# A joint gate/up block's products in a fixed order, a longer trail for the second token half, and a new buffer layout in both feed-forward phases

## The chip, the cores and the metric

The kernel runs on one core of one Trainium2 chip, as a single launch. The metric is the device time of the launch in microseconds (us). The engines named below are TensorE (PE: the matmuls; PEld: its weight loads), VectorE (DVE), ScalarE (ACT), GpSimd (POOL) and SyncE (SP, which here issues the loads of weights). Each engine runs its own instructions in a fixed order; an instruction that has to wait holds up those behind it on the same engine. DMA transfers run beside them.

## The reference

One decoder layer on 256 tokens of width 2048, in float32:

```
x <- LN1(alpha*x + 0.5*SwiGLU_1(x))                  # FFN 1, inner width 5632
x <- LN2(alpha*x + W_out [DiffAttn(x) || RWKV7(x)])  # the mixers
x <- LN3(alpha*x + 0.5*SwiGLU_2(x))                  # FFN 2, inner width 5632
swiglu(x) = (silu(x @ w_gate) * (x @ w_up)) @ w_down
```

`alpha` is 2 to the power 1/4, and each LN is a layer norm with gain and bias over the 2048 columns. The change does not touch the inside of the mixers.

## The kernel before

**Split numbers.** Each float32 factor is split into a high part in the matmul's format (fp32r) and the rest, the low part. A product of one 128-row piece of weights with one token half (128 tokens, 512 output columns) is three matmuls that add into the same bank: high x high, high x low, low x high (L130, L131, L132). The halves of the tokens are transposed and kept as `xh`, `xl`; those of the inner activations as `hh`.

**A tile of weights.** SP loads up to three 128-row pieces as `raw` (L114; 8 buffers in an FFN). ACT casts them to the high part `wh` (L122), and DVE subtracts to get the low part `wl` (L123). There are NW pairs of `wh`/`wl` buffers, 4 in an FFN, used in turn. A cast into a buffer waits until PE has finished the last product that reads it.

**Plain blocks.** `Stream.block` streams the tiles of 512 output columns. The first token half's product runs as a tile arrives; the second half's product trails by LAG tiles (`pend`), one tile in an FFN. The first block of gate and of up, and all of the down projection, run so. Each FFN is worked off in two parts over the inner width: six and five column blocks of gate and up, then four column blocks of down over them.

**Joint blocks.** The other ten column blocks of gate and up in each FFN run in `two_blocks`, which computes gate and up for both token halves together and saves products over the first six pieces by a scheme of sums and differences (Winograd's). The sums of activations for it (`comb`, tiles `xs`, `xsh`, `xsl`) are made once per FFN by `combinations`, L284 to L292. A joint block opens with six products of nine matmuls each. They are called P1 to P6 below, in the order of the code:

- P1 (L170): bank a, from tile r11 of the gate weights.
- P2 (L173): bank z, from the difference r12 - r11 that DVE makes in place (L172).
- P3 (L178): bank u, which ACT has filled with a copy of a (L174), from r22 less that difference (DVE, L177).
- P4 (L183): bank a again, from r21.
- P5 (L185): bank w, which ACT has filled with a copy of u after P3 (L181), from r22 - r12 (DVE, L176).
- P6 (L187): bank u again, after DVE has added s5, a copy of z, to it (L184).

After them come the other ten pieces in plain form, each tile for both token halves. There are 20 joint blocks. Four of them open a stretch: the first of each half of each FFN. The other 16 follow another joint block and are called ordinary.

**Norms.** When a down block of the second half ends, DVE adds it to `y` (L351) and takes statistics (L352). After the fourth, `ln_tail` aggregates them (L240), applies the norm in two passes of four pieces (L248, L249), and PE transposes each piece through a bank `tr` (L76), or DMA stores it (L251 at the end; L254 for the residual).

**Order.** The code is recorded and then put in order by a list scheduler that simulates the engines. It may move an instruction ahead of others on its engine as far as data and buffers allow; what it decides is fixed in the program.

Of the kernel before, what the change touches and what calls it, by code (L numbers as in the profile page):

```python
# [10 lines left out]
F32 = mybir.dt.float32  # L11
# [5 lines left out]
P = 128  # L17
# [12 lines left out]
SCALE = 64 ** -0.5  # L30
LAG = {"ffn": 1, "mix": 2}
NW = {"ffn": 4, "mix": 5}
# [8 lines left out]
def build(tc, A, out):  # L41
# [31 lines left out]
    def transpose_split(src, tt, q, store, on_dve=False):  # L73
        tr = tr_bank[-1]()
# [15 lines left out]
    class Stream:  # L90
# [9 lines left out]
        def phase(self, name, pool, banks=None):  # L100
            assert not self.pend
            self.name, self.pool, self.banks, self.slot, self.rot = name, pool, banks, 0, 0
            self.wide = WIDE[name]

# [12 lines left out]
        def halves(self, raw, n, w=NB, g=None):  # L117
            wh, wl = (self.pool.tile([P, self.wide, NB], F32R, tag=f"{t}{self.slot}", name=nm(t)) for t in ("wh", "wl"))
            self.slot = (self.slot + 1) % NW[self.name]
            for k in range(0, n, g or n):  # L120
                c = slice(k, k + (g or n))
                SC.copy(out=wh[:, c, :w], in_=raw[:, c, :w])  # L122
                V.tensor_tensor(out=wl[:, c, :w], in0=raw[:, c, :w], in1=wh[:, c, :w].bitcast(F32), op=ALU.subtract)  # L123
            return wh, wl

        def product(self, acc, lhs, n, wh, wl, first, last, w=NB):
            a = acc[:, :w]
            for j in range(n):
                hi, lo = lhs(j)
                T.matmul(a, hi, wh[:, j, :w], start=first and j == 0, stop=False, skip_group_check=True)  # L130
                T.matmul(a, hi, wl[:, j, :w], start=False, stop=False, skip_group_check=True)  # L131
                T.matmul(a, lo, wh[:, j, :w], start=False, stop=last and j == n - 1, skip_group_check=True)  # L132

# [10 lines left out]
        def block(self, src, c0, w, ks, lhs, done, wide=None):  # L144
            blk = dict(ks=ks, w=w, lhs=lhs, done=done)
            wide = wide or self.wide
            ki = 0
            while ki < len(ks):
                left = len(ks) - ki
                n = wide if left % wide == 0 or left > 2 * wide else min(2, left)  # L150
                for f in self.hooks.get(self.step, ()):
                    f()
                self.step += 1
                g = 1 if self.step == 1 else None
                raw = self.load(src, ks[ki][0], n, c0, w, g)
                st = (blk, ki, n) + self.halves(raw, n, w, g)
                self.mm(st, 0)
                self.pend.append(st)
                if len(self.pend) > max(0, min(LAG[self.name], self.step // 4 - 1)):
                    self.mm(self.pend.pop(0), 1)  # L160
                self.run_bg()
                ki += n

        def two_blocks(self, srcs, c0, x, comb, done):
# [12 lines left out]
            V.tensor_tensor(out=r11, in0=r22, in1=r11, op=ALU.subtract)  # L177
            self.product(u, comb(1), 3, *self.halves(r11, 3), False, False)  # L178
            s5 = self.pool.tile([P, NB], F32, tag="s5", name=nm("s5"))
            SC.copy(out=s5, in_=z)  # L180
            SC.copy(out=w, in_=u)  # L181
            r21 = self.load(s0, 3, 3, c0)
            self.product(a, A12, 3, *self.halves(r21, 3), False, False)  # L183
            V.tensor_tensor(out=u, in0=u, in1=s5, op=ALU.add)  # L184
# [87 lines left out]
    def ffn(fp, wg, wu, wd, lg, lb, res, last, extra=None):  # L272
# [5 lines left out]
        def combinations():  # L278
# [10 lines left out]
            V.tensor_tensor(out=sr[:, 3], in0=x12, in1=sr[:, 1], op=ALU.subtract)  # L289
            sh, sl = (fp.tile([P, 4, 3, P], F32R, tag=t, name=nm(t)) for t in ("xsh", "xsl"))  # L290
            SC.copy(out=sh, in_=sr)
            V.tensor_tensor(out=sl, in0=sr, in1=sh.bitcast(F32), op=ALU.subtract)  # L292
            return lambda i: lambda j: (sh[:, i, j, :], sl[:, i, j, :])
        for half, nj in enumerate((6, 5)):
# [118 lines left out]
    def mix(mp, pq, C):  # L413
# [567 lines left out]
    def ffn_bank(pool):  # L981
        return lambda: pool.tile([P, 4, P], F32, tag="tr", name=nm("tr"), bufs=2)

    with tc.tile_pool(name="fp1", bufs=1, reuse_waits="tile") as fp, tc.tile_pool(name="pt1", bufs=1, space=bass.MemoryType.PSUM, reuse_waits="tile") as pt:
        tr_bank.append(ffn_bank(pt))
        stream.phase("ffn", fp, pt)
        xc = [fp.tile([P, D], F32, tag=f"y{tt}", name=nm("xc")) for tt in range(2)]

# [59 lines left out]
```

## Time and profile before

| | |
|---|---|
| three runs | 2017.73 us median, 2016.71 to 2018.85 |
| the profiled execution | 2017.31 us, of which the span from first to last instruction is 2015.2 |
| mean granted TensorE clock | 0.983 of full |
| PE, PEld, DVE, ACT, POOL busy | 96%, 79%, 68%, 48%, 2% of the span |
| matmuls, weight loads | 9491 each |
| read from memory | 364 MB, at 184 GB/s over the span |

A row of the timeline gives the start in us from the span's start, the time it took, the engine, the line of the program, the operation with its output and inputs, the size, the number of instructions taken together, and in brackets how long the engine had been idle before it and what released it. A row of the waits gives the total, the number of times and the longest, in us. A row of the windows gives the stretch, its length, the busy time of PE, PEld, DVE, ACT and POOL with their instruction counts, the granted TensorE clock, the share of the DMA engines' time, and GB/s. A matmul's time in a row is from start to end, while the next begins earlier; the distance of starts is what a stream of them takes.

### The profile page before, as it was taken

What the parts mean: (1) busy time and instruction counts of PE and PEld (TensorE: products, weight loads), DVE (VectorE), ACT (ScalarE), POOL (GpSimd) and SP (SyncE); (2) the same over time, 40 slices, a digit from 0 to 9 for tenths busy, and PEclk for the clock granted to TensorE, in tenths of its full rate; (3) what the DMA queues carried; (4) which work ended last, traced back from release to release, by engine and by line L of the source; (5) the groups of instructions that cost most, each with busy time, mean ns of one, the idle gap of its engine ahead of it and who ended that gap; (6) DMA issues with size and microseconds to landing.
All of it is one profiled execution on the core that took longest, in us unless ns stands there. A gap on an engine that the chain in (4) does not pass through costs nothing. (4 is left out here: it accounts for less than half of the span.)

```text
span 2015.2 us, 24059 instructions
## 1 busy us (share of the span) xinstructions
PE 1944.6 (96%) x9491; PEld 1585.4 (79%) x9491; DVE 1377.2 (68%) x1477; ACT 971.0 (48%) x1078; POOL 43.5 (2%) x76
## 2 busy tenths in 40 slices
PE   9999999999999989999999988899999999999997
PEld 7787888887888868877778766778878888878885
DVE  6888744578775565776777768667885447888455
ACT  5565543355554325645574543445554334555431
POOL 0200000000000000000000000000000000000000
PEclk9999999999999979999999999889999999999998
DMA  9546566545667426555445634855457565456851
GB/s 323 180 168 208 198 246 218 174 167 199 203 201 264 147 91 193 166 152 164 130 133 161 185 131 127 277 165 172 167 191 258 206 212 177 167 180 206 268 193 42
DMA packets 200465, 373.27 MB, mean 185 GB/s; under 512 B 20778, under 2 KB 22896, under 8 KB 200096
## 3 DMA queue, kind: packets, MB, share of 16 engines
q1 hardware_dynamic: 180688, 350.52, 52.0%
q10 hardware_dynamic: 17440, 14.29, 2.5%
q0 software_dynamic: 2224, 6.93, 1.3%
q8 instruction: 74, 1.21, 0.2%
q14 instruction: 39, 0.32, 0.0%
HBM read 364.10 MB, written 7.60 MB: 184 GB/s over the span
## 5 line engine op out<-in xcount | busy, mean ns | idle before, releaser
L123 DVE TENSOR_TENSOR wl<-raw,wh 128x1536 fp32r<-128x1536 f32 (+3 forms) x585 | 881.8, 1522 | 511.9 <-ACT wh L122 510.0
L122 ACT CAST wh<-raw 128x1536 fp32r<-128x1536 f32 (+3 forms) x585 | 750.7, 1294 | 802.4 <-PE acc L132 638.0
L131 PE MATMUL acc<-wl,xh 128*128 128x512 f32 (+1 forms) x1652 | 644.2, 392 | 6.4 <-DVE wl L123 6.4
L132 PE MATMUL acc<-wh,xl 128*128 128x512 f32 (+1 forms) x1652 | 641.4, 390 | 0.0
L130 PE MATMUL acc<-wh,xh 128*128 128x512 f32 (+1 forms) x1652 | 636.0, 393 | 3.1 <-ACT wh L122 3.1
L131 PEld LDWEIGHTS acc<-wl,xh 128*128 128x128 f32 x1652 | 312.0, 189 | 72.6 <-DVE wl L123 8.3
L130 PEld LDWEIGHTS acc<-wh,xh 128*128 128x128 f32 x1652 | 312.4, 189 | 69.9 <-ACT wh L122 4.9
L132 PEld LDWEIGHTS acc<-wh,xl 128*128 128x128 f32 x1652 | 312.1, 189 | 64.6 <-issue 1.7
L131 PE MATMUL acc<-wl,hh 128*128 128x512 f32 x704 | 274.4, 390 | 0.0
L132 PE MATMUL acc<-wh,hh 128*128 128x512 f32 x704 | 274.2, 390 | 0.0
L130 PE MATMUL acc<-wh,hh 128*128 128x512 f32 x704 | 270.1, 389 | 0.0
L131 PEld LDWEIGHTS acc<-wl,hh 128*128 128x128 f32 x704 | 132.1, 188 | 27.5
L132 PEld LDWEIGHTS acc<-wh,hh 128*128 128x128 f32 x704 | 132.2, 188 | 27.3
L130 PEld LDWEIGHTS acc<-wh,hh 128*128 128x128 f32 x704 | 132.1, 188 | 27.2
L130 PE MATMUL acc<-wh,xsh 128*128 128x512 f32 x240 | 100.6, 419 | 14.6 <-ACT acc L181 13.2
L131 PE MATMUL acc<-wl,xsh 128*128 128x512 f32 x240 | 95.4, 398 | 3.6 <-DVE wl L123 3.6
L132 PE MATMUL acc<-wh,xsl 128*128 128x512 f32 x240 | 95.2, 397 | 0.0
L130 PEld LDWEIGHTS acc<-wh,xsh 128*128 128x128 f32 x240 | 45.8, 191 | 35.7 <-ACT acc L181 21.9
L131 PEld LDWEIGHTS acc<-wl,xsh 128*128 128x128 f32 x240 | 46.1, 192 | 12.8 <-DVE wl L123 4.4
L132 PEld LDWEIGHTS acc<-wh,xsl 128*128 128x128 f32 x240 | 46.0, 192 | 10.3
L300 ACT ACTIVATE sg<-acc 128x512 f32<-128x512 f32 x44 | 26.2, 599 | 20.3 <-PE acc L132 20.2
L172 DVE TENSOR_TENSOR raw<-raw,raw 128x1536 f32<-128x1536 f32 x20 | 35.2, 1758 | 0.7
(263 smaller groups left out, 1104.1 us busy)
## 6 DMA issues: line engine op xcount, KB each, us to landing
raw<-in_ffn_w_down_dram SPq DMA_DIRECT2D x112, 768.0 KB, 4.3
raw<-in_ffn_w_up_dram SPq DMA_DIRECT2D x88, 768.0 KB, 6.2
raw<-in_ffn_w_gate_dram SPq DMA_DIRECT2D x80, 768.0 KB, 6.4
raw<-in_w_in_dram SPq DMA_DIRECT2D x96, 512.0 KB, 3.6
raw<-in_ffn_w_gate_dram SPq DMA_DIRECT2D x55, 512.0 KB, 4.7
raw<-in_ffn_w_up_dram SPq DMA_DIRECT2D x44, 512.0 KB, 5.2
raw<-in_w_out_dram SPq DMA_DIRECT2D x32, 512.0 KB, 3.8
raw<-in_ffn_w_down_dram SPq DMA_DIRECT2D x8, 512.0 KB, 3.6
```

The source lines that it names most:

```text
L122: SC.copy(out=wh[:, c, :w], in_=raw[:, c, :w])
L123: V.tensor_tensor(out=wl[:, c, :w], in0=raw[:, c, :w], in1=wh[:, c, :w].bitcast(F32), op=ALU.subtract)
L130: T.matmul(a, hi, wh[:, j, :w], start=first and j == 0, stop=False, skip_group_check=True)
L131: T.matmul(a, hi, wl[:, j, :w], start=False, stop=False, skip_group_check=True)
L132: T.matmul(a, lo, wh[:, j, :w], start=False, stop=last and j == n - 1, skip_group_check=True)
L172: V.tensor_tensor(out=r11, in0=r12, in1=r11, op=ALU.subtract)
L300: SC.activation(out=s, in_=acc, func=AF.Silu)
```

## The change

- `two_blocks`: the order edge `tc.issue_after(i)` puts P4's matmuls behind the last matmul of P3. The casts and differences are recorded as before.
- `LAG` in an FFN is 2 instead of 1. In the first gate and up block's gate part, and in the down projection of the second half, it is 3, with 5 pairs of `wh`/`wl` buffers instead of 4. The trail builds up by one tile for every two steps at the start.
- FFN 2's first gate block uses tiles three pieces wide, not two.
- `ffn_layout` claims the FFN's buffers in one given order (raw, combination halves, s5, sg, h, y) before any is used, which moves them; the split combinations get tags of their own.
- Two of three transposes of a norm use a spare accumulator bank in place of the two `tr` banks.

```
-LAG = {"ffn": 1, "mix": 2}
+LAG = {"ffn": 2, "mix": 2}
...
-                if len(self.pend) > max(0, min(LAG[self.name], self.step // 4 - 1)):
+                while len(self.pend) > max(0, min(self.lag, (self.step - 1) // 2)):
                     self.mm(self.pend.pop(0), 1)
...
-            self.product(u, comb(1), 3, *self.halves(r11, 3), False, False)
+            i = self.product(u, comb(1), 3, *self.halves(r11, 3), False, False)
...
             r21 = self.load(s0, 3, 3, c0)
-            self.product(a, A12, 3, *self.halves(r21, 3), False, False)
+            h = self.halves(r21, 3)
+            with tc.issue_after(i):
+                self.product(a, A12, 3, *h, False, False)
...
-                    stream.block(wg, c0, NB, KX, x_lhs, gate_done, 2)
+                    stream.buffers(5, 3)
+                    stream.block(wg, c0, NB, KX, x_lhs, gate_done, 3 if last else 2)
+                    stream.buffers(4, 2)
...
             if half == 1:
                 gb = load_gb_over_x(lg, lb)
+                stream.buffers(5, 3)
...
+        def bank(spare=False):
+            n[0] += 1
+            if spare and n[0] % 3:
+                i = (stream.rot + n[0] % 3) % NACC["ffn"]
+                return (pa if i < 3 else pool).tile([P, 4, P], F32, tag=f"acc{i}", name=nm("tr"))
+            return pool.tile([P, 4, P], F32, tag="tr", name=nm("tr"), bufs=2)
...
+    def ffn_layout(fp):
+        for tag, n in (("raw", NRAW["ffn"]), ("wh4", 1), ("wl4", 1)):
+            fp.tile([P, 3, NB], F32, tag=tag, name=nm(tag), bufs=n)
+        for tag, n in (("s5", 1), ("sg", 2), ("h", 2)):
+            fp.tile([P, NB], F32, tag=tag, name=nm(tag), bufs=n)
+        for t in range(2):
+            fp.tile([P, D], F32, tag=f"y{t}", name=nm("y"))
```

The lines that the prediction names move by a few: L122 and L123 become L125 and L126, L130 to L132 become L133 to L135, L172, L177, L181, L184 and L188 become L176, L181, L185, L190 and L194, L351 becomes L360, L284 becomes L290.

PE in an ordinary joint block (the second of FFN 1), from the transposes that stand between P2 and P3. Before; `wh_153` is P3's tile and `wh_157` P4's:

```order
L308 MATMUL tr_137_774<-ident_73,h_136_772 128x128 x4
L308 MATMUL tr_140_790<-ident_73,h_139_788 128x128 x4
L130 MATMUL acc_143_799<-wh_153_838,xsh_58_327 128x512
L130 MATMUL acc_141_797<-wh_157_856,xh_6_98 128x512
L131 MATMUL acc_141_797<-wl_158_857,xh_6_98 128x512
L132 MATMUL acc_141_797<-wh_157_856,xl_7_99 128x512
```

The changed program at the same place; `wh_161` is P3's tile:

```order
L314 MATMUL tr_145_782<-ident_73,h_144_780 128x128 x4
L314 MATMUL tr_148_798<-ident_73,h_147_796 128x128 x4
L133 MATMUL acc_151_807<-wh_161_846,wh4_66_323 128x512
L134 MATMUL acc_151_807<-wl_162_847,wh4_66_323 128x512
L135 MATMUL acc_151_807<-wh_161_846,wl4_67_324 128x512
L133 MATMUL acc_151_807<-wh_161_846,wh4_66_323 128x512
```

Before, P4 starts after one matmul of P3, and the other eight follow it; now all nine of P3 stand before P4. DVE's and ACT's rows of this block, from the cast of its first tile to the addition to u, are in the same order in both programs.

DVE in FFN 1's first joint block, from L177 on. Before; `wl_103` belongs to P4, `wl_105` to P5, `wl_99` to P3, `wl_107` to P6:

```order
L177 TENSOR_TENSOR raw_91_497<-raw_97_529,raw_91_497 128x1536
L123 TENSOR_TENSOR wl_103_552<-raw_101_549,wh_102_551 128x1536
L123 TENSOR_TENSOR wl_105_566<-raw_94_512,wh_104_565 128x1536
L319 TENSOR_TENSOR hh_83_468<-tr_82_463,hh_83_468 128x512
L123 TENSOR_TENSOR wl_99_534<-raw_91_497,wh_98_533 128x1536
L123 TENSOR_TENSOR wl_107_580<-raw_97_529,wh_106_579 128x1536
```

The change; `wl_111` belongs to P4, `wl_113` to P5, `wl_115` to P6 and `wl_107` to P3:

```order
L126 TENSOR_TENSOR wl_111_560<-raw_109_557,wh_110_559 128x1536
L325 TENSOR_TENSOR hh_91_467<-tr_90_462,hh_91_467 128x512
L181 TENSOR_TENSOR raw_99_505<-raw_105_537,raw_99_505 128x1536
L126 TENSOR_TENSOR wl_113_574<-raw_102_520,wh_112_573 128x1536
L325 TENSOR_TENSOR hh_91_467<-tr_93_493,hh_91_467 128x512
L126 TENSOR_TENSOR wl_115_588<-raw_105_537,wh_114_587 128x1536
L126 TENSOR_TENSOR wl_107_542<-raw_99_505,wh_106_541 128x1536
```

P3's low half moved from before P6's to behind it, while on PE P3 moved ahead of P4 as above.

DVE in the first joint block of FFN 1's second half, from L177 on. Before; `wl_496`, `wl_492`, `wl_498` belong to P4, P3, P5:

```order
L177 TENSOR_TENSOR raw_484_2877<-raw_490_2909,raw_484_2877 128x1536
L349 SCALAR_TENSOR_TENSOR y_365_2021<-rc_478_2868,acc_458_2701 128x512
L123 TENSOR_TENSOR wl_496_2932<-raw_494_2929,wh_495_2931 128x1536
L123 TENSOR_TENSOR wl_492_2914<-raw_484_2877,wh_491_2913 128x1536
L123 TENSOR_TENSOR wl_498_2946<-raw_487_2892,wh_497_2945 128x1536
```

The change; `wl_504`, `wl_506`, `wl_500` belong to P4, P5, P3:

```order
L358 SCALAR_TENSOR_TENSOR y_373_2029<-rc_486_2876,acc_469_2724 128x512
L181 TENSOR_TENSOR raw_492_2885<-raw_498_2917,raw_492_2885 128x1536
L126 TENSOR_TENSOR wl_504_2940<-raw_502_2937,wh_503_2939 128x1536
L126 TENSOR_TENSOR wl_506_2954<-raw_495_2900,wh_505_2953 128x1536
L126 TENSOR_TENSOR wl_500_2922<-raw_492_2885,wh_499_2921 128x1536
```

P3's low half now stands behind P5's. FFN 2's second half has the same rows in the same order, and FFN 2's first joint block has P3's low half behind P6's in both programs. On PE, the matmuls between the last use of the buffer that a block's first tile goes into and that block's P1 are 41 before and 27 now in FFN 1's first joint block, 45 and 36 in the first of each second half, 33 and 32 in FFN 2's first, and 42 and 42 in an ordinary one. After the last product of the first token half, 14 matmuls of the second follow before a norm, and now 22.

More of the change, by code (lines that the diff above doesn't have):

```diff
@@ L73, in transpose_split @@
     def transpose_split(src, tt, q, store, on_dve=False):
-        tr = tr_bank[-1]()
+        tr = tr_bank[-1](True)
         for j in range(4):
@@ L102, in phase, with buffers @@
             self.name, self.pool, self.banks, self.slot, self.rot = name, pool, banks, 0, 0
-            self.wide = WIDE[name]
+            self.wide, self.lag, self.nw = WIDE[name], LAG[name], NW[name]
+        def buffers(self, nw, lag):
+            self.nw, self.lag, self.slot = nw, lag, self.slot % nw
         def bank(self):
@@ L118, in halves @@
             wh, wl = (self.pool.tile([P, self.wide, NB], F32R, tag=f"{t}{self.slot}", name=nm(t)) for t in ("wh", "wl"))
-            self.slot = (self.slot + 1) % NW[self.name]
+            self.slot = (self.slot + 1) % self.nw
             for k in range(0, n, g or n):
@@ L131, in product @@
                 T.matmul(a, hi, wl[:, j, :w], start=False, stop=False, skip_group_check=True)
-                T.matmul(a, lo, wh[:, j, :w], start=False, stop=last and j == n - 1, skip_group_check=True)
+                i = T.matmul(a, lo, wh[:, j, :w], start=False, stop=last and j == n - 1, skip_group_check=True)
+            return i.ins
         def mm(self, st, tt):
@@ L289, in combinations @@
             V.tensor_tensor(out=sr[:, 3], in0=x12, in1=sr[:, 1], op=ALU.subtract)
-            sh, sl = (fp.tile([P, 4, 3, P], F32R, tag=t, name=nm(t)) for t in ("xsh", "xsl"))
+            sh, sl = (fp.tile([P, 4, 3, P], F32R, tag=t, name=nm(t)) for t in ("wh4", "wl4"))
             SC.copy(out=sh, in_=sr)
@@ L947, in mix, with mix_bank @@
         rot = [0]
-        def mix_bank():
+        def mix_bank(spare=False):
             rot[0] += 1
@@ L981, in ffn_bank @@
     def ffn_bank(pool):
-        return lambda: pool.tile([P, 4, P], F32, tag="tr", name=nm("tr"), bufs=2)
+        n = [0]
+        def bank(spare=False):
[4 more added lines that the diff above has]
+            return pool.tile([P, 4, P], F32, tag="tr", name=nm("tr"), bufs=2)
+        return bank
+    def ffn_layout(fp):
[5 more added lines that the diff above has]
+            fp.tile([P, D], F32, tag=f"y{t}", name=nm("y"))
     with tc.tile_pool(name="fp1", bufs=1, reuse_waits="tile") as fp, tc.tile_pool(name="pt1", bufs=1, space=bass.MemoryType.PSUM, reuse_waits="tile") as pt:
@@ L986, in build @@
         stream.phase("ffn", fp, pt)
+        ffn_layout(fp)
         xc = [fp.tile([P, D], F32, tag=f"y{tt}", name=nm("xc")) for tt in range(2)]
@@ L1007, in build @@
         stream.phase("ffn", fp, pt)
+        ffn_layout(fp)
         ffn(fp, A["ffn2_w_gate"][0], A["ffn2_w_up"][0], A["ffn2_w_down"][0], A["ln3_g"], A["ln3_b"], xs, True)
```

## The prediction, made before the changed kernel was run

> **What bounds the kernel now.** I read the page's busy shares first, then the waits, then the timeline of one joint block.
>
> ```profile
> PE 1944.6 (96%) x9491; PEld 1585.4 (79%) x9491; DVE 1377.2 (68%) x1477; ACT 971.0 (48%) x1078; POOL 43.5 (2%) x76
> ...
> PE acc L130 <- ACT acc L181: 13.2, 20, 0.7
> ...
> 1985.02 0.39 PE L132 MATMUL acc<-wh,hh 128*128 128x512 f32 x1
> ...
> 1994.54 0.39 PE L132 MATMUL acc<-wh,hh 128*128 128x512 f32 x1
> ```
>
> TensorE (PE) is busy 96% of the span, so whatever moves the time must move PE's idle time or its clock. The third line says that in each of the 20 joint blocks PE stands 0.66 us (13.2 over 20) for the copy of u into w. The last two rows are 42 matmuls apart: 9.52 / 42 = 0.227 us a matmul, so a nine-matmul product takes 2.04 us. The share does not say what ends second there. In the joint block at 90 to 112 us:
>
> ```profile
> 89.88 1.48 ACT L122 CAST wh<-raw 128x1536 fp32r<-128x1536 f32 x1 [1.03 <-PE acc L132]
> 91.39 1.76 DVE L123 TENSOR_TENSOR wl<-raw,wh 128x1536 fp32r<-128x1536 f32 x1 [2.17 <-ACT wh L122]
> 93.18 1.76 DVE L172 TENSOR_TENSOR raw<-raw,raw 128x1536 f32<-128x1536 f32 x1
> 94.97 1.76 DVE L176 TENSOR_TENSOR raw<-raw,raw 128x1536 f32<-128x1536 f32 x1
> ...
> 98.32 0.68 DVE L305 SCALAR_TENSOR_TENSOR h<-sg,acc 128x512 f32<-128x512 f32 x1
> 98.92 1.75 DVE L177 TENSOR_TENSOR raw<-raw,raw 128x1536 f32<-128x1536 f32 x1
> 101.18 5.09 DVE L123 TENSOR_TENSOR wl<-raw,wh 128x1536 fp32r<-128x1536 f32 x3
> 106.19 1.75 DVE L188 TENSOR_TENSOR raw<-raw,raw 128x1536 f32<-128x1536 f32 x1
> 110.73 0.68 DVE L184 TENSOR_TENSOR acc<-acc,s 128x512 f32<-128x512 f32 x1
> 109.10 0.50 PE L130 MATMUL acc<-wh,xsh 128*128 128x512 f32 x1 [0.66 <-ACT acc L181]
> 111.47 0.19 PEld L130 LDWEIGHTS acc<-wh,xsh 128*128 128x128 f32 x1 [0.22 <-DVE acc L184]
> ```
>
> The cast of the block's first tile starts when PE frees its buffer. From then VectorE (DVE) runs without a stop until the addition u += s5 at L184 ends at 111.41, and P6, which needs it, loads its weights at 111.47 after waiting 0.22 us. So PE waits twice, and the second wait is the end of a full DVE queue. From the rows: 1.51 us from the cast to the first difference, 1.79 for each of the next two steps, then 1.67 for a wide operation (101.18 to 106.19 is three) and 0.60 for a narrow one (98.32 to 98.92).
>
> **The edge in the 16 ordinary joint blocks.** The copy now runs under P4, and PE is spared that stop: 0.66 us idle and the slower restart (0.50 for the first matmul, not 0.39 as at 1985.02), an estimate of 0.8 in all. But DVE's and ScalarE's (ACT's) orders between cast and L184 are as before, and 42 matmuls stand between the freed buffer and P1 both times. P6 can start no earlier than 111.5, so PE waits there for what it no longer waits before P5. Gain: nothing I can price; bounds -0.2 us a block (the 0.22 above) and +0.3 (a second restart, since the one stop becomes two, before P3's low half and before P6). I take 0, and -3 to +5 for all 16.
>
> **The edge in the four opening blocks.** There DVE has the low half of P3 after P4's and P5's (in the first block of each FFN after P6's too). Before, P4 could fill PE meanwhile; now P3 has to come first, and P4, P5 and P6 stand in PE's queue behind it. The second FFN's first block has this DVE order already before the change:
>
> ```profile
> 1309.16 1.48 ACT L122 CAST wh<-raw 128x1536 fp32r<-128x1536 f32 x1 [3.02 <-PE acc L132]
> ...
> 1326.55 1.75 DVE L123 TENSOR_TENSOR wl<-raw,wh 128x1536 fp32r<-128x1536 f32 x1
> ...
> 1328.35 0.80 PE L131 MATMUL acc<-wl,xsh 128*128 128x512 f32 x1 [2.77 <-DVE wl L123]
> ...
> 1337.22 0.61 PE L130 MATMUL acc<-wh,xsh 128*128 128x512 f32 x1
> ```
>
> P3's low half was ready 19.14 us after the cast (1328.30), and PE had waited though P4 was already done.
>
> First block of the first FFN:
>
> ```profile
> 45.55 1.48 ACT L122 CAST wh<-raw 128x1536 fp32r<-128x1536 f32 x1 [3.21 <-PE acc L132]
> ...
> 56.68 0.39 PE L130 MATMUL acc<-wh,xsh 128*128 128x512 f32 x1
> ...
> 68.14 0.39 PE L130 MATMUL acc<-wh,xsh 128*128 128x512 f32 x1
> ```
>
> P2 starts at 56.68, so P1 at 54.64; nothing ahead of it moves PE. Before, 41 matmuls lay between the freed buffer and P1 (9.31 us: 45.33, the cast 0.22 later). With the longer trail 27 lie there: 54.64 - 6.13 + 0.22 = 48.73 for the cast. To the end of P3's low half DVE has 1.51 + 1.79 + 1.79 + six wide operations at 1.67 + three narrow at 0.60 + 1.75 for the last: 18.7, near the 19.14 above (one narrow more there): so 67.4. P3's eight other matmuls, P4 and P5 take 5.9: P6 at 73.3. Before it came at 68.14 with one matmul put ahead, 67.9. **+5.4 us** (4.5 to 6.5), with PE idle from about 59.7 to 67.4 but for one matmul.
>
> First block of each second half:
>
> ```profile
> 394.75 1.48 ACT L122 CAST wh<-raw 128x1536 fp32r<-128x1536 f32 x1 [2.60 <-PE acc L132]
> ...
> 404.75 0.39 PE L130 MATMUL acc<-wh,xh 128*128 128x512 f32 x1
> ...
> 416.13 0.39 PE L130 MATMUL acc<-wh,xsh 128*128 128x512 f32 x1
> ```
>
> P1 at 404.75; 45 matmuls from the freed buffer before, 36 after: cast at 404.75 - 8.17 + 0.22 = 396.8. DVE: 1.51 + 1.79 + 1.79 + five wide + two narrow + 1.75 = 16.4 (P5's low half now ahead of P3's), so 413.2; P6 at 413.2 + 5.9 = 419.1 against 415.9. **+3.2 us**, twice (2.2 to 4.2 each). PE is idle from 408.8 to 413.2 but for one matmul near 411.
>
> Second FFN's first block: the cast comes 0.2 us later (32 matmuls, not 33), P3 at 1328.5, P4 behind it, P6 at 1334.4 at full clock; before it was at 1336.8, the way from P3 at half clock. With the cut below, 1336.9: **0** (-1.5 to +1.5).
>
> **The clock.** Windows of 3.41 us on the grid that the clock steps by:
>
> ```profile
> 730.13:733.54 3.41, 1.19 (x7) 0.72 (x6) 3.41 (x6) 0.00 (x0) 0.74 (x1) 1.00 0.07 26
> 733.54:736.96 3.42, 1.63 (x8) 0.86 (x6) 3.42 (x7) 1.17 (x2) 0.00 (x0) 0.50 0.75 260
> 1030.50:1033.91 3.41, 1.89 (x9) 1.58 (x10) 3.38 (x8) 1.65 (x6) 0.00 (x0) 1.00 0.23 43
> 1324.05:1327.46 3.41, 0.50 (x1) 0.19 (x1) 3.41 (x4) 0.97 (x1) 0.00 (x0) 1.00 0.74 240
> 1334.29:1337.70 3.41, 3.41 (x10) 2.64 (x9) 2.29 (x2) 0.66 (x1) 0.00 (x0) 0.50 0.71 189
> ```
>
> A window with PE busy 35% or less is followed by half clock, one with 55% is not; from 1334.29 a whole window is busy at half clock, and the next one, from 1337.7, is granted full clock again. Four idle microseconds with one matmul in them put at least 1.9 into one window, 44% busy or less: between the bounds, in most positions under 35%. So I count a cut in both second-half blocks and in the first. It lasts from the restart to the end of a full window, 3.4 to 6.8 us, and half of that is lost: 1.7 to 3.4, taken as 2.5. Three times: **+7.5 us** (0 to 10).
>
> The Trainium skill ("TensorE: Matmul & The Clock Gate", "Why this matters for your kernels") asks only that no gap pass about 3 us. In the second-half blocks each of the two gaps is some 2.1, so by that rule there is no cut there. The trace leans against it: at 1324.05 one matmul stands between two gaps of which the longer is 2.77, and the clock halves.
>
> **The longer trail at the norms.** At the end of both FFNs, 22 second-half matmuls instead of 14 follow the first half's last one. In the last norm:
>
> ```profile
> 1997.23 0.69 DVE L351 TENSOR_TENSOR y<-y,acc 128x512 f32<-128x512 f32 x1 [6.47 <-PE acc L132]
> ...
> 1999.98 0.39 PE L132 MATMUL acc<-wh,hh 128*128 128x512 f32 x1
> ...
> 2004.95 0.69 DVE L352 BATCH_NORM_STATS2 st<-y 128x6 f32<-128x512 f32 x1
> ```
>
> DVE runs from 1997.23 to the end without a stop, so the chain starts 8 x 0.227 = **1.8 us** sooner against PE's last matmul (0.5 to 2). The first norm has the same chain:
>
> ```profile
> 727.87 0.69 DVE L351 TENSOR_TENSOR y<-y,acc 128x512 f32<-128x512 f32 x1 [6.47 <-PE acc L132]
> ...
> 748.17 0.85 PE L130 MATMUL acc<-wh,xh 128*128 128x288 f32 x2 [1.25 <-ACT wh L122]
> ```
>
> Its transposes no longer wait for a bank, and the first mixer load no longer for the norm, but the same DVE work stands between: **-1.8** (-4 to 0). In the down phases PE never stops, so trailing hides nothing there.
>
> **The new layout before the second FFN.**
>
> ```profile
> 1263.29 0.33 ACTq L254 DMA_DIRECT2D xs<-y  x1
> 1265.36 1.02 DVE L284 TENSOR_TENSOR xs<-xh,xl 128x512 f32<-128x512 f32 x2
> 1269.36 1.22 DVE L123 TENSOR_TENSOR wl<-raw,wh 128x1024 fp32r<-128x1024 f32 x1
> 1270.63 0.80 PE L131 MATMUL acc<-wl,xh 128*128 128x512 f32 x1 [2.84 <-DVE wl L123]
> ...
> xs<-y ACTq DMA_DIRECT2D x8, 256.0 KB, 2.8
> ```
>
> The sums now lie over y, which the last store, issued at 1263.29, still reads: 1263.3 + 2.8 + the next sum gives 1266.3, 0.9 later. The first low half is three tiles wide (1.75, not 1.22) and behind one more sum (0.47): +1.0. **+1.9** (0 to 4).
>
> **Sum.** 5.4 + 3.2 x 2 + 7.5 - 1.8 - 1.8 + 1.9 = 17.6, on the profiled execution's 2017.3 (span 2015.2 and 2.1 around it; 0.4 under the median): 2034.9, so 2035.
>
> **Rivals.** *The edge does what it says* (the faster side). It decides where L190 ends before P5 does, which in an ordinary block takes DVE 0.8 us sooner against PE; then 20 stops of 0.8 go and the trail gives 3.6: 2017.3 - 16 - 3.6 + 1.9 = 1999.6. For it: the 13.2 us in the waits. Against it: the 0.22 us wait on L184 right behind the stop. 5%. *Openings as priced, but no cut in the second-half blocks:* one matmul between two gaps of 2.1 us keeps the clock up, as the 55% window at 1030.50 did: 2035 - 5 = 2030. 15%. The rule of the Trainium skill's clock page named above would give this one. *Openings cost little:* if the cast does not wait for the buffer as long as counted, half of the 11.8 and no cut: 2017.3 + 5.9 - 1.7 = 2021.5. 8%. *The ordinary blocks lose too,* from where P3's low half, 104.5 in the block above, comes 0.3 us after its need: +5, 2040. 10%. *Nothing net,* gains at norms and start balancing one opening: 2017. 7%.
>
> **How the numbers follow.** The forecast has 55%. The range 2019 to 2043 takes in the neighbours and the unknown clock. A measurement here tells about 0.2%, 4 us: faster 7%, same 8%, slower 85%.
>
> **What would show it.** In the changed profile: PE's waits for L181's copy gone; in ordinary blocks a wait of about 0.7 us for L190 in their place; in the first block near 60 to 67 us a wait for P3's cast and then its low half, 7 us together; around 411 and its twin in the second FFN about 4; half clock behind them. If ordinary blocks come 0.8 us closer together than before, or the openings show under 2 us of idle time, the forecast is wrong.

## The result, and the profile after

The changed kernel takes 2040.94 us in the median of three runs (2039.96 to 2044.69), against 2017.73 before: a ratio of 1.0119, interval 1.0096 to 1.0142. It is slower, by 23 us; 2035 had been forecast. The profiled execution's span is 2039.2 us against 2015.2, so the two traces hold 24.0 us to be explained.

First the page's busy shares and three rows of PE's waits, of the changed kernel, then two rows of the waits before:

```profile
PE 1951.4 (96%) x9491; PEld 1590.2 (78%) x9491; DVE 1377.2 (68%) x1475; ACT 971.6 (48%) x1076; POOL 42.8 (2%) x76
...
PE acc L134 <- DVE wl L126: 23.5, 10, 7.6
PE acc L133 <- ACT wh L125: 13.2, 7, 3.5
PE acc L133 <- DVE acc L190: 6.5, 16, 0.4
```

```profile
PE acc L131 <- DVE wl L123: 10.0, 6, 2.8
PE acc L130 <- ACT wh L122: 4.5, 4, 1.6
```

The 13.2 us for the copy of u are gone from the waits. In their place stand 6.5 us for the addition (L190), in the 16 ordinary blocks. The waits for low halves have grown from 10.0 to 23.5 us, the longest 7.6, and those for casts from 4.5 to 13.2 (the same figure as the copy's by accident). DVE is busy as long as before (1377.2 us), PE 6.8 us longer with as many matmuls: no work was added, it is waiting and clock.

Where the 24 us arise can be read without any wait: take the same instruction in both traces and see how far it has moved. The marks are the start of the first subtraction (L172, now L176) in a joint block, numbered 1 to 20, and of the matmuls or transposes named. Times are in us.

| stretch | before | after | change | the sum had |
|---|---|---|---|---|
| start to block 2 (FFN 1's opening) | 93.18 | 100.93 | +7.75 | 5.4 + 2.5 |
| three ordinary blocks, 2 to 5 | 130.41 | 130.43 | 0.0 | 0 |
| 5 to 7 (second half's opening) | 217.59 | 222.33 | +4.74 | 3.2 + 2.5 |
| 7 to 10, ordinary | 130.39 | 130.40 | 0.0 | 0 |
| 10 to the first mixer matmul (norm 1) | 176.60 | 173.71 | -2.9 | -1.8 |
| mixers, to norm 2's first transpose | 503.21 | 509.92 | **+6.7** | nothing |
| to FFN 2's first low-half matmul | 19.25 | 23.87 | **+4.6** | 1.9 |
| to block 12 (FFN 2's opening) | 91.91 | 89.98 | -1.9 | 0 |
| 12 to 15, ordinary | 130.59 | 130.39 | -0.2 | 0 |
| 15 to 17 (second half's opening) | 217.47 | 223.59 | +6.1 | 3.2 + 2.5 |
| 17 to 20, ordinary | 130.37 | 130.44 | +0.1 | 0 |
| 20 to the end | 174.24 | 173.17 | -1.1 | -1.8 |

The changes add up to 24.0. The timeline of PE shows the openings and an ordinary block (in `acc<-wh,wh` the second name is a combination half, which has buffers of that name in the new layout):

```profile
63.03 0.80 PE L133 MATMUL acc<-wh,wh 128*128 128x512 f32 x1 [3.42 <-ACT wh L125]
67.02 0.79 PE L134 MATMUL acc<-wl,wh 128*128 128x512 f32 x1 [3.19 <-DVE wl L126]
...
119.22 0.50 PE L133 MATMUL acc<-wh,wh 128*128 128x512 f32 x1 [0.41 <-DVE acc L190]
...
418.15 0.50 PE L133 MATMUL acc<-wh,wh 128*128 128x512 f32 x1 [1.39 <-ACT wh L125]
420.89 0.79 PE L134 MATMUL acc<-wl,wh 128*128 128x512 f32 x1 [2.24 <-DVE wl L126]
...
1698.58 0.50 PE L133 MATMUL acc<-wh,wh 128*128 128x512 f32 x1 [1.38 <-ACT wh L125]
1701.33 0.79 PE L134 MATMUL acc<-wl,wh 128*128 128x512 f32 x1 [2.25 <-DVE wl L126]
```

Each of these three openings has the pair of waits foreseen, for P3's cast and then for its low half, 6.6 us in the first block and 3.6 in the second halves. The windows on the clock's grid show what follows them:

```profile
62.33:65.74 3.41, 0.80 (x1) 0.29 (x1) 3.41 (x4) 0.65 (x1) 3.41 (x7) 0.50 0.40 106
...
417.31:420.73 3.42, 0.50 (x1) 0.19 (x1) 3.42 (x3) 2.64 (x3) 0.00 (x0) 1.00 0.15 20
420.73:424.14 3.41, 3.25 (x8) 2.58 (x9) 3.41 (x3) 0.00 (x0) 0.00 (x0) 0.50 0.72 229
424.14:427.55 3.41, 3.41 (x17) 2.81 (x16) 1.75 (x3) 2.94 (x3) 0.00 (x0) 1.00 0.97 331
1697.31:1700.73 3.42, 0.50 (x1) 0.19 (x1) 3.42 (x3) 3.08 (x3) 0.00 (x0) 1.00 0.04 5
1700.73:1704.14 3.41, 2.81 (x7) 2.23 (x8) 3.41 (x3) 0.00 (x0) 0.00 (x0) 0.50 0.73 231
1704.14:1707.56 3.42, 3.42 (x10) 2.65 (x9) 1.60 (x3) 1.96 (x2) 0.00 (x0) 0.50 0.98 315
1202.38:1205.80 3.42, 1.39 (x18) 0.93 (x18) 2.56 (x12) 0.25 (x1) 1.11 (x1) 1.00 0.00 0
1205.80:1209.22 3.42, 2.98 (x21) 2.38 (x22) 2.48 (x7) 1.38 (x3) 0.00 (x0) 0.50 0.00 0
1209.22:1212.63 3.41, 3.41 (x9) 2.64 (x9) 0.32 (x1) 0.13 (x1) 0.00 (x0) 0.50 0.00 0
```

All three openings are cut, that is, run at half clock behind their waits: the first from 62.3 to 72.6 us, three windows. In the second halves one cut lasts one window, the other two: half of a window, 1.7 us, is about the difference between +4.74 and +6.1. In run 9 below, with the same code in these blocks, the two windows fall in FFN 1 and the one in FFN 2, and the stretches take 223.37 and 222.05 us: the difference belongs to the clock, not to the block.

The last three windows lie where the prediction had no term, at the end of the mixers. PE's waits there, after:

```profile
1206.06 0.66 PE L924 MATMUL at<-ident,ot 128*128 128x128 f32 x2 [1.85 <-DVE ot L920]
...
1238.82 0.53 PE L133 MATMUL acc<-wh,xh 128*128 128x512 f32 x1 [0.35 <-DVE y L971]
1243.73 0.50 PE L133 MATMUL acc<-wh,xh 128*128 128x512 f32 x1 [1.83 <-ACT xh L82]
1245.95 0.50 PE L134 MATMUL acc<-wl,xh 128*128 128x512 f32 x1 [0.63 <-DVE wl L126]
```

and before:

```profile
1196.44 0.68 PE L736 MATMUL sm<-Rs,TT 64*64 64x64 f32 x16 [0.80 <-DVE Rs L730]
```

No line of the change touches this code: L911, L730 and L737 before are L920, L739 and L746 after. But the list scheduler put it in another order. DVE's order before (`ot` is the last head of the attention, `Rs`, `SV` and `BK` belong to the other mixer's scan, `y` and `wl` to the projection):

```
977 L916 TENSOR_SCALAR qq<-at_9429,ng 128x256
978 L730 COPY Rs_8579<-sm_8570 128x256
979 L908 TENSOR_TENSOR ars_9363<-ars_9363,fl_9362 128x4
980 L909 TENSOR_TENSOR ars_9363<-ars_9363 128x2
981 L911 TENSOR_SCALAR ot_9359<-at_9355,ars_9363 128x128 x2
982 L737 COPY SV_7975<-sm_8599 64x4x64
```

and after:

```
977 L917 TENSOR_TENSOR ars_9371<-ars_9371,fl_9370 128x4
978 L918 TENSOR_TENSOR ars_9371<-ars_9371 128x2
979 L925 TENSOR_SCALAR qq<-at_9437,ng 128x256
980 L920 TENSOR_SCALAR ot_9367<-at_9363,ars_9371 128x128 x2
981 L739 COPY Rs_8587<-sm_8578 128x256
```

After, `ot` goes ahead of `Rs`, the scan's last step falls behind the projection, and its result, the last input of the mixers, comes late: 1.85 + 0.35 + 1.83 + 0.63 of waits in place of 0.80, and a window of 41% (1.39 of 3.42) followed by two at half clock.

The other surprise is the start of FFN 2. Rows of the timeline after, then the DMA issues of the last store, after and before:

```profile
1279.63 0.33 ACTq L260 DMA_DIRECT2D xs<-y  x1
...
1285.18 1.03 DVE L290 TENSOR_TENSOR xs<-xh,xl 128x512 f32<-128x512 f32 x2 [3.40 <-DMA xs<-y]
...
1291.59 0.80 PE L134 MATMUL acc<-wl,xh 128*128 128x512 f32 x1 [7.60 <-DVE wl L126]
```

```profile
xs<-y ACTq DMA_DIRECT2D x1, 256.0 KB, 5.3
```

```profile
xs<-y ACTq DMA_DIRECT2D x1, 256.0 KB, 3.0
```

The sums wait for the store that reads the buffer they now lie in, as foreseen; but the store took 5.3 us to land, not 2.8 to 3.0. PE then waits 7.60 us for the first low half, where it had waited 2.84 before.

### The profile page after: what moved, and what is told of

Its sections match the earlier page's. It is cut to its first block, busy times and chain, and to the rows that moved or that the text cites. A ratio compares the mean times of both kernels' runs of the same rounds, so it can differ in the third digit from the quotient of the medians.

```text
span 2039.2 us, 24058 instructions
## 1 busy us (share of the span) xinstructions
PE 1951.4 (96%) x9491; PEld 1590.2 (78%) x9491; DVE 1377.2 (68%) x1475; ACT 971.6 (48%) x1076; POOL 42.8 (2%) x76
## 5 line engine op out<-in xcount | busy, mean ns | idle before, releaser
L126 DVE TENSOR_TENSOR wl<-raw,wh 128x1536 fp32r<-128x1536 f32 (+3 forms) x583 | 881.6, 1528 | 506.2 <-ACT wh L125 503.4
L125 ACT CAST wh<-raw 128x1536 fp32r<-128x1536 f32 (+3 forms) x583 | 752.4, 1298 | 829.9 <-PE acc L135 693.3
L135 PE MATMUL acc<-wh,xl 128*128 128x512 f32 (+1 forms) x1652 | 643.2, 391 | 0.1
L133 PE MATMUL acc<-wh,xh 128*128 128x512 f32 (+1 forms) x1652 | 637.0, 394 | 5.9 <-ACT wh L125 3.6
L133 PEld LDWEIGHTS acc<-wh,xh 128*128 128x128 f32 x1652 | 313.4, 190 | 74.2 <-ACT wh L125 4.6
L135 PEld LDWEIGHTS acc<-wh,xl 128*128 128x128 f32 x1652 | 312.7, 189 | 65.2 <-issue 1.7
L133 PE MATMUL acc<-wh,hh 128*128 128x512 f32 x704 | 268.3, 389 | 0.0
L135 PE MATMUL acc<-wh,hh 128*128 128x512 f32 x704 | 265.3, 389 | 0.0
L134 PE MATMUL acc<-wl,hh 128*128 128x512 f32 x704 | 264.5, 390 | 0.0
L133 PEld LDWEIGHTS acc<-wh,hh 128*128 128x128 f32 x704 | 132.1, 188 | 27.3
L135 PEld LDWEIGHTS acc<-wh,hh 128*128 128x128 f32 x704 | 132.2, 188 | 27.3
L133 PE MATMUL acc<-wh,wh 128*128 128x512 f32 x240 | 99.6, 415 | 16.1 <-ACT wh L125 9.7
L134 PE MATMUL acc<-wl,wh 128*128 128x512 f32 x240 | 99.0, 412 | 12.8 <-DVE wl L126 11.0
L135 PE MATMUL acc<-wh,wl 128*128 128x512 f32 x240 | 96.4, 402 | 0.0
L133 PEld LDWEIGHTS acc<-wh,wh 128*128 128x128 f32 x240 | 46.3, 193 | 33.1 <-DVE acc L190 13.2
L134 PEld LDWEIGHTS acc<-wl,wh 128*128 128x128 f32 x240 | 46.6, 194 | 28.1 <-DVE wl L126 19.5
L135 PEld LDWEIGHTS acc<-wh,wl 128*128 128x128 f32 x240 | 46.8, 195 | 9.4
L311 DVE SCALAR_TENSOR_TENSOR h<-sg,acc 128x512 f32<-128x512 f32 x44 | 30.0, 682 | 9.7 <-PE acc L135 9.7
```

The source lines that it names most:

```text
L135: i = T.matmul(a, lo, wh[:, j, :w], start=False, stop=last and j == n - 1, skip_group_check=True)
L311: V.scalar_tensor_tensor(out=h, in0=sg[tt], scalar=0.5, in1=acc, op0=ALU.mult, op1=ALU.mult)
```

## Experiments

All medians are in us; ratios are to the kernel before, which ran again beside each group of runs (medians 2017.8 to 2018.4), with 95% intervals.

| run | median | ratio |
|---|---|---|
| 1 edge alone | 2018.81 | 1.0006 (0.9996 to 1.0016) |
| 2 changed, no edge | 2035.88 | 1.0086 (1.0069 to 1.0103) |
| 3 changed, short trail | 2022.57 | 1.0022 (1.0012 to 1.0031) |
| 4 changed, old layout in FFN 2 | 2037.44 | 1.0097 (1.0082 to 1.0113) |
| 5 before, L188 later | 2021.14 | 1.0013 (1.0004 to 1.0023) |
| 6 before, edge and two reorderings | 2030.18 | 1.0051 (1.0036 to 1.0067) |
| 7 changed, r21 later | 2048.65 | 1.0139 (1.0122 to 1.0156) |
| 8 combination | 2028.63 | 1.0050 (1.0035 to 1.0065) |
| 9 changed, mixers' end held | 2037.99 | 1.0099 (1.0086 to 1.0112) |
| 10 edge, L188 behind the next tile | 2011.07 | 0.9970 (0.9961 to 0.9980) |
| 11 the same, no edge | 2015.04 | 0.9989 (0.9980 to 0.9998) |
| 12 as 10, openings mended | 2002.87 | **0.9929** (0.9913 to 0.9944) |

The theory at the start was the prediction's: no gain in ordinary blocks, since the end of DVE's queue stands right behind the copy; the loss in the openings, by edge and trail together. The rivals: the edge is itself the loss, or the layout is.

**1. The edge alone**, on the kernel before:

```
-            self.product(a, A12, 3, *self.halves(r21, 3), False, False)
+            h = self.halves(r21, 3)
+            with tc.issue_after(i):
+                self.product(a, A12, 3, *h, False, False)
```

> The kernel before with the order edge alone (P4 behind the last matmul of P3); trail, layout, spare banks as before. Theory (in ordinary joint blocks VectorE's queue ends at the addition to u at the same time, so the stop for the copy only changes its place): 16 ordinary blocks 0; the first block of FFN 1 loses about 1, and 2.5 more if its idle piece of some 3 us falls into one clock window; the others about 0. 2018 to 2021 us. Rival (the edge is worth its 16 us, and the rest of the change gives them back and more): about 2002 us.

No measurable change. The ordinary blocks moved by +0.01 each (130.44 for three), and the wait is the one foreseen:

```profile
157.51 0.50 PE L130 MATMUL acc<-wh,xsh 128*128 128x512 f32 x1 [0.41 <-DVE acc L187]
```

FFN 1's opening lost 2.5 us, the second halves' 0.1 each; the total stays level because FFN 2's opening took 1.6 us less and the mixers 1.2 less, these with DVE's order there unchanged. A stretch can so move by about 1 us with no edit of its own.

**2. The changed kernel without the edge:**

```
-            with tc.issue_after(i):
-                self.product(a, A12, 3, *h, False, False)
+            self.product(a, A12, 3, *h, False, False)
```

> The changed kernel without the order edge; the longer trail, layout and spare banks stay. Theory (two things meet at the openings: the cast comes later because of the trail, and P4 may not fill the gap because of the edge): each of four openings gets back one product of 2.0 less the copy's stop of 0.8, that is 1.2, and the shorter idle pieces (about 2 us in place of 4 at the second halves) spare two half-clock windows of about 1.7 each; ordinary blocks 0. About 2033 us, 2030 to 2037. Rival (the edge alone costs what was lost): about 2020 us. Rival (the edge has no part in it): 2041 us.

2035.88, where about 2033 was expected. 5 us of the loss by the medians need the edge (9.5 by the profiled executions, but that of this run is 4.4 us under its median). Most sits where the edge meets the trail: from the first subtraction of the second half's first block to the next block the edge alone (run 1) adds 0.12, the rest of the change without the edge 0.11, the two together 2.70; in FFN 2 0.12, 0.12 and 4.12. Run 3 will show that of this rest it is the trail. The 2.0 by which that first subtraction comes later is there without the edge. In FFN 1's opening the kernel with the trail and no edge loses 7.0 of the 7.75, which the theory had put down to the edge.

**3. The changed kernel with the short trail:**

```
-LAG = {"ffn": 2, "mix": 2}
+LAG = {"ffn": 1, "mix": 2}
...
-                stream.buffers(5, 3)
```

(both calls of `buffers(5, 3)` and the one that sets it back).

> The changed kernel with the trail of one tile and 4 buffer pairs everywhere, as before; edge, layout, spare banks and the wide gate tiles stay. Theory: at the openings 41 and 45 matmuls stand again between the freed buffer and P1, so the openings of both second halves lose nothing (10.9 back) and that of FFN 1 about 2 (5.7 back); the norms lose what the trail gave them (+3.9); the order at the mixers' end is nearly that of before again (6 back). About 2022 us, 2019 to 2027. Rival (the openings lose by the edge, whatever the trail): 2035 us or more.

18.4 of the 23 us go, 17.3 of span. But only some 12 of these lie in the openings and norms; the mixers, whose trail the change leaves at 2, also gave back 5.1 of their 6.7. The openings of the second halves now lose 0.1 each, with edge and layout still in place. That the mixers moved asked for an explanation of its own, the reordering shown above.

**4. The old layout in FFN 2:**

```
-        ffn_layout(fp)
```

> The changed kernel without the given layout in FFN 2 only, so that the sums of activations no longer lie over the rows that the residual stores still read. Theory (VectorE's 3.4 us wait for these stores is what the layout costs there): the start of FFN 2 gets 3.4 back, 2037.5 us. Rival (the wider gate tiles and their loads set that start): 2041 us, with the first low half as late as now.

2037.44, the number expected. The stretch to FFN 2's first low half falls from +4.6 to +1.1, so the wait for the store is 3.5.

**5. Is the mixers' order alone worth its 6.7?** The new theory: any edit that moves the scheduler to that order costs it. In the kernel before, L188 goes behind the addition of L184, which happens to bring about the order of after; no edge, trail or layout:

```
-            V.tensor_tensor(out=u, in0=u, in1=s5, op=ALU.add)
+            iu = V.tensor_tensor(out=u, in0=u, in1=s5, op=ALU.add).ins
...
-            V.tensor_tensor(out=r11, in0=r21, in1=r11, op=ALU.subtract)
+            with tc.issue_after(iu):
+                V.tensor_tensor(out=r11, in0=r21, in1=r11, op=ALU.subtract)
```

> The kernel before, with L188 (r11 = r21 - r11) issued behind the addition u += s5 instead of ahead of it in each joint block; neither edge, trail nor layout. The scheduler then also orders the end of the mixers otherwise: ot and the y of the projection ahead of the scan's SV and BK, as in the changed kernel. Theory (the mixers' tail loses some 6.7 us by this order alone, whatever part of a change brings it about): the stretch from the last transposes of ot to the second norm's first transposes grows by 5 to 7.5 us, the 16 ordinary blocks gain up to 0.2 each because P6 waits less for the addition, so about 2021 (2018 to 2025). Rival (the loss belongs to the longer trail's buffers or to the spare banks): the tail moves by under 1.5 us, so about 2014 to 2017.

2021.14, where 2021 was expected. The mixers took 6.2 us longer with the same waits, of which two:

```profile
1194.94 0.66 PE L916 MATMUL at<-ident,ot 128*128 128x128 f32 x2 [1.85 <-DVE ot L912]
...
1232.57 0.50 PE L130 MATMUL acc<-wh,xh 128*128 128x512 f32 x1 [1.88 <-ACT xh L82]
```

Three ordinary blocks took 130.02 instead of 130.41, 0.13 less each.

**6. Can the edge gain if DVE's queue is shorter?** The kernel before with the edge, L188 behind the addition, and r21's halves behind P3's low half:

```
+            with tc.issue_after(self.low):
+                h = self.halves(r21, 3)
```

> The kernel before with the edge, and VectorE's queue in a joint block shortened at the two places where PE waits in it: L188 behind the addition u += s5, and the cast and low half of r21 (P4's) behind the low half of P3. Trail and layout as before; the mixers' end in the order of before. Theory (the edge gains nothing in the ordinary blocks because P6 then waits for the addition, the end of a full VectorE queue; one wide operation of 1.7 us less ahead of it lets PE run through): the ordinary blocks come 0.4 to 0.7 us closer together each, 43.47 to about 42.9, the openings cost less by about 1 us each, so about 2004 (1998 to 2010). Rival (ordinary blocks are bound elsewhere, by when PE frees the buffers or by ScalarE): spacing stays at 43.4 and the time is 2014 to 2019.

A miss: 2030, and an ordinary block takes 44.27 us instead of 43.47. DVE and PE in one of them:

```profile
148.61 6.77 DVE L123 TENSOR_TENSOR wl<-raw,wh 128x1536 fp32r<-128x1536 f32 x4 [1.07 <-ACT wh L122]
...
157.23 0.50 PE L131 MATMUL acc<-wh,xsh 128*128 128x512 f32 x1 [0.29 <-DVE acc L189]
160.56 0.50 PE L132 MATMUL acc<-wl,xh 128*128 128x512 f32 x1 [0.99 <-DVE wl L123]
```

With P3's halves first in its order, DVE stands 1.07 us for their cast, where it had r21's low half to do; and the tile after P6's gets its low half late, since L188 is now ahead of it. Each reordering had only passed the wait on. FFN 2's opening did gain, 3.6 us from its first subtraction to the next block's.

**7. The same r21 edit in the changed kernel**, after which the scheduler orders the mixers' end as before:

> The changed kernel with the cast and low half of r21 (P4's) issued behind the low half of P3 in each joint block; the mixers' end is then ordered as in the kernel before. Theory: the mixers' tail gives back its 5 to 7 us, and P3's low half comes one wide operation (1.7 us) sooner in the openings of FFN 1 and of both second halves, so these give back 1.7 each and perhaps a half-clock window: about 2041 - 6 - 5 = 2030 (2025 to 2034). Rival (the tail's loss does not come from that order): 2035 to 2038.

A miss in the total, 2048.65. Of the two faults just shown this edit has the one on r21: the addition comes later, PE waits 1.32 us for it instead of 0.41, and an ordinary block takes 44.65. The openings of the second halves still lose 3.2 us each from one subtraction to the next (2.7 and 4.1 before this edit), not 1.7 less. But the part on the mixers holds: with trail, edge and layout in place their stretch is 0.5 us longer than before, not 6.7, with PE's last wait for `Rs` as before the change:

```profile
1214.61 0.91 PE L747 MATMUL sm<-Rs,TT 64*64 64x64 f32 x16 [0.80 <-DVE Rs L741]
```

**8. A combination:** the changed kernel with both reorderings, `LAG` 1, `buffers(4, 2)` in the last half of down and the old layout in FFN 2.

> The changed kernel with the two reorderings of VectorE's queue (L194 behind the addition; r21's cast and low half behind P3's low half), a trail of one tile again in gate, up and the first half of down, the last half of down with buffers (4, 2), and the spare banks and new layout in FFN 1 only. Theory: as the kernel before with edge and shortened queue (about 2004), and the first norm still starts sooner, 1 to 3 us: about 2002 (1996 to 2008). Rival (the ordinary blocks do not gain): 2012 to 2018.

2028.63, above both ranges: its ordinary blocks lose 0.8 each as in run 6.

**9. The mixers' end held in the old order** by two order edges in the changed kernel (the scan's last matmul and its copy SV are kept in `scan`):

```
+                with tc.issue_after(scan["mm"]) if end else ExitStack():
                     for qb in range(2):
                         T.transpose(tr[:, qb, :], ot[:, qb, :], ident)
+                with tc.issue_after(scan["sv"]) if end else ExitStack():
                     V.tensor_scalar(out=q[:, h, :],
```

> The changed kernel, and only the end of the mixers put back in the order of the kernel before, by two order edges: the last transposes of ot behind the scan's last matmul, and the copy qq behind the scan's copy SV. Theory (the term that the prediction lacks is this order): the stretch from the last transposes of ot to the second norm's first transposes gives back 6 to 7.5 us and nothing else moves: 2034 (2031 to 2037). Rival (the tail is longer because of something else that the longer trail does there): over 2038.

2037.99, between the theory and its rival: 2.8 of the 6.7 us come back. The edges hold the scan ahead of the projection but leave `Rs` behind `ot` on DVE, and PE now waits for it, at half clock behind:

```profile
1209.01 1.12 PE L745 MATMUL sm<-Rs,TT 64*64 64x64 f32 x16 [2.44 <-DVE Rs L739]
```

Runs 5 and 7 show that the order costs the 6 us, give or take the 1 us by which run 1 moved; this one, that two edges are not the old order.

**10. L188 one place further back.** Run 6 named both faults. So: r21 where it was, L188 behind the low half of the tile that follows P6's, its product behind both halves of that tile, and the two edges of run 9:

```
-            V.tensor_tensor(out=r11, in0=r21, in1=r11, op=ALU.subtract)
...
+                    if i == 0 and k == 6:
+                        with tc.issue_after(self.low):
+                            V.tensor_tensor(out=r11, in0=r21, in1=r11, op=ALU.subtract)
```

**11. The same without the edge**, and **12. the same with the openings mended**: no edge in FFN 1's first joint block, r21's halves behind P3's low half in FFN 2's first:

```
+            with tc.issue_after(self.low) if late else ExitStack():
+                h = self.halves(r21, 3)
+            with tc.issue_after(i) if edge else ExitStack():
```

> The kernel before with the edge; L188 (r11 = r21 - r11) recorded and issued behind the low half of the tile after P6's, with its product behind both halves of that tile; the mixers' end held in the order of before by the two order edges. No longer trail, no layout. Theory (in the ordinary blocks the edge gains nothing because P6 then waits 0.4 us for the addition at the end of a full VectorE queue; L188 is 1.67 us of that queue and nothing needs it so soon): P6's wait goes, and no low half is late behind it, so the ordinary blocks come 0.4 to 0.6 us closer, 43.47 to about 42.95, 16 times: 2018.8 - 8.3 = 2010.5 (2007 to 2014). Rival (another resource stands right behind: P3's low half, or the buffers that the casts wait for): 2015 to 2019.

> The same without the edge: L188 behind that low half, the mixers' end held in its order. Theory (the 0.66 us stop for the copy of u stays, the shorter queue alone frees only the 0.2 us wait that stood behind it): 2018.4 - 16 x 0.2 = 2015 (2012 to 2017), so that the edge is worth 3 to 6 us once the queue is shorter. Rival (the queue was all of it, and the edge adds nothing even then): as the run with the edge, within 1 us.

> The run with the edge and the later L188, and two changes in opening blocks: no edge in the first block of FFN 1 (the edge alone lost 2.5 us there), and in the first block of FFN 2 the cast and low half of r21 behind the low half of P3 (that block came 3.6 us nearer to the next one where it was tried). Theory: 2010.5 - 2.5 - 2.5 = 2005.5 (2002 to 2010). Rival (what an opening gains is made up by its next wait): as the run with the edge, 2010.

2011.07, 2015.04 and 2002.87: the first two within 0.6 us of the number expected, the last 2.6 better. Three ordinary blocks take 128.35 with the edge (42.78 each) and 129.99 without (43.33). DVE in such a block of run 10, and PE's only wait in it:

```profile
110.09 1.28 DVE L325 TENSOR_TENSOR hh<-tr,hh 128x512 fp32r<-128x512 f32 x2
111.29 0.69 DVE L188 TENSOR_TENSOR acc<-acc,s 128x512 f32<-128x512 f32 x1
111.89 1.75 DVE L123 TENSOR_TENSOR wl<-raw,wh 128x1536 fp32r<-128x1536 f32 x1
113.55 1.75 DVE L199 TENSOR_TENSOR raw<-raw,raw 128x1536 f32<-128x1536 f32 x1
```

```profile
106.89 0.50 PE L132 MATMUL acc<-wl,xsh 128*128 128x512 f32 x1 [0.15 <-DVE wl L123]
```

The addition is no longer behind the subtraction (now L199), PE's wait for it is gone, and 0.15 is left for P3's low half. So the edge is worth 0.55 us in an ordinary block once the queue is shorter, and 0.0 when it is not (run 1). Over all it is worth 4 us, since FFN 1's opening takes 2.8 back and the mixers, whose DVE order the scheduler turned at their end once more, 1.4; run 12 saves the first by leaving the edge out there. With 2002.87 run 12 is 0.7% faster than the kernel before. In FFN 2's opening it gained 6.5 us where run 6 gained 3.6, with the same two waits left; the last section says why. The 2.6 us by which it beat the number expected are about the 2.9 us that the clock's grid gave there, which is luck and not forecast.

## Why the prediction was right, and where it was not

The forecast, slower by 17 us at 2035, had the sign and most of the size; the measured 2041 lies in its range. The openings came about as told; that the total came this near is partly luck, since 9.4 us that were missing or priced too low met 3.1 that came out lower.

- **Ordinary blocks, 0.** Right: 0.0 to 0.1 in three of the four stretches, -0.2 in the other. The reason is shown too: in runs 10 and 11 the same edge gains when the addition at the end of DVE's queue comes sooner, and not otherwise. The wait expected at 0.7 was 0.41: what the copy had cost beyond that, PE spends at the other short stop, before P3's low half. The rival "the ordinary blocks lose too" has the nearest number, 2040, but not the reason: they lost nothing.
- **FFN 1's first block, 5.4 + 2.5.** Measured 7.75. The size was right, and P3's low half reached PE at 67.0 us where 67.4 was forecast. The attribution was not: the part is headed with the edge, but the edge alone costs 2.5, the change without it 7.0.
- **Second halves, 3.2 + 2.5 each.** Measured 4.74 and 6.1; both clocks were cut, so the rival without a cut (2030) is out, as are 2021.5 and 2017. Runs 1 and 2 show that it takes edge and trail together.
- **FFN 2's first block, 0 (-1.5 to +1.5).** Measured -1.9, just outside. Half of it, 1.0, arises ahead of the block's first subtraction, where the half clock of the start ends 2.9 us behind the mark, not 5.7; in the block the clock is cut for two windows (from 1345.7 us), not three as before (from 1327.5).
- **Norms, -1.8 twice.** Measured -2.9 (within -4 to 0) and -1.1.
- **The layout before FFN 2, 1.9 (0 to 4).** Mis-sized: 4.6, past its bound. The term took 2.8 us for the last store to land; it took 5.3. Of the 4.6, run 4 gives 3.5 to the layout. The other 1.1 compares with the 1.0 that the sum had for the wider first low half, but no run took that alone. In run 4 the last store was as slow, 5.2 us, but nothing waited for it.
- **The mixers, no term.** The step that failed: the sum priced only code that the diff touches. The order that the scheduler gave the mixers' end had changed, and its rows were there to be compared. It cost 6.7, of which 6.2 come with the order alone (run 5); with the trail but the old order (run 7) it was 0.5.

The last two, 6.7 and 2.7, less 3.1 for the terms that came out lower, are the 6.4 us by which the spans differ beyond 17.6. Why the trail's or L188's place turns the scheduler at the far end of the mixers was not traced.

## What to carry to other kernels

Where a scheduler sets the order, compare it over the whole program, also where the diff touches nothing: an order that has flipped has to be priced like an edit. An edge that takes a wait away gains only if what ends second has moved too; find it, shorten that queue, and look once more at what has now become late. Where a trail or an edge passes through blocks that begin a stretch, price these apart from the others.

## What the hardware showed

**The clock goes by the share of a window, not by the length of a gap.** Runs 6 and 12 have the same two waits in FFN 2's opening. PE's timeline of run 6, then of run 12:

```profile
1334.11 0.49 PE L131 MATMUL acc<-wh,xsh 128*128 128x512 f32 x1 [0.95 <-ACT wh L122]
1336.32 0.80 PE L132 MATMUL acc<-wl,xsh 128*128 128x512 f32 x1 [1.71 <-DVE wl L123]
```

```profile
1315.98 0.49 PE L131 MATMUL acc<-wh,xsh 128*128 128x512 f32 x1 [0.95 <-ACT wh L122]
1318.19 0.50 PE L132 MATMUL acc<-wl,xsh 128*128 128x512 f32 x1 [1.71 <-DVE wl L123]
```

In run 6 they fall into one window of the clock's grid, in run 12 the boundary at 1316.31 parts them. The windows of run 6, then of run 12:

```profile
1332.21:1335.62 3.41, 1.44 (x8) 0.77 (x6) 3.38 (x3) 3.41 (x4) 0.00 (x0) 1.00 0.13 18
1335.62:1339.03 3.41, 2.71 (x6) 2.15 (x7) 3.41 (x3) 0.78 (x2) 0.00 (x0) 0.50 0.59 213
```

```profile
1312.90:1316.31 3.41, 2.46 (x13) 1.73 (x11) 3.15 (x3) 3.41 (x5) 0.00 (x0) 1.00 0.00 0
1316.31:1319.73 3.42, 1.71 (x8) 1.28 (x8) 3.42 (x4) 1.96 (x3) 0.00 (x0) 1.00 0.74 229
1319.73:1323.14 3.41, 3.41 (x17) 2.82 (x16) 3.41 (x5) 1.97 (x2) 0.00 (x0) 1.00 0.12 23
```

42% busy (1.44 of 3.41) was followed by half clock, 50% (1.71 of 3.42) was not. Run 12 also has L188 elsewhere, so run 8, with both reorderings of run 6, is the closer comparison: its waits there are 0.96 and 1.70, a boundary parts them into windows of 2.08 us busy each (61%), no cut follows, and the block takes 43.61 us to the next, against 46.45 in run 6 and 43.60 in run 12. The 2.9 us are where the grid happened to lie. An edit far ahead can move them, and perhaps another execution too: the six of run 12 took 1998.8 to 2008.5 us, and the profiled one is the shortest.

The prediction's bounds were 35 and 55%. All fourteen traces together, from 8 us on, narrow them, but not to a point. Each of the 95 windows at full clock that were under 43% busy was followed by half clock, and none above 53.5% was; of the 25 between, 15 were. A window of run 10 and one of run 1:

```profile
1319.49:1322.91 3.42, 1.47 (x9) 1.01 (x7) 3.42 (x3) 3.35 (x6) 0.00 (x0) 1.00 0.00 0
1322.91:1326.32 3.41, 0.50 (x1) 0.19 (x1) 3.41 (x5) 1.47 (x2) 0.00 (x0) 1.00 0.55 168
```

```profile
60.59:64.00 3.41, 1.69 (x6) 1.21 (x7) 3.41 (x3) 2.31 (x3) 3.41 (x7) 1.00 0.68 193
64.00:67.42 3.42, 3.42 (x10) 2.65 (x9) 3.31 (x4) 1.79 (x2) 2.53 (x6) 0.50 0.67 198
```

43% was not cut in the first, 49% was in the second; what decides between them stays open. The way back is stricter: after a window at half clock the least share that brought full clock was 79% (2.69 of 3.42, run 11 at 1260.67). It is no sharp bound either. In the changed kernel 87% (2.98 of 3.42, at 1205.80) was followed by half clock and 95% (3.25 of 3.41, at 420.73) was not, and in run 8 a full window of the mixers' small matmuls (3.42 of 3.42, at 1193.73) was followed by half clock again. The Trainium skill ("TensorE: Matmul & The Clock Gate", "Why this matters for your kernels") asks that no gap pass about 3 us. The trace does not agree: gaps of 1.39 and 2.24 with one matmul between them brought a cut at 420.73.

**The last stores of norm 2 took longer to land.** The last one took 5.3 us in the changed kernel and 3.0 at the same place before. The traces of the other runs narrow this down. The last four stores took 4.9 to 6.3 us in the changed kernel and in all six built on it, also without the edge (run 2), with the short trail (run 3) and with the old layout in FFN 2 (runs 4 and 8); they took 2.4 to 4.3 us in the kernel before and in all six built on that. So none of these three is the reason. What the changed kernel and those six share includes the wider tiles of FFN 2's first gate block (loads of 768 KB instead of 512 beside the stores), the spare banks and the layout in FFN 1. No run took these one by one, so the reason stays open.
